# Gla's last two levels of scores as blocks, its small products behind Q's, and retention's out product between the value units

## The chip, the cores and the metric

The program runs on one core of one Trainium2 chip. Its time is the device time of one execution in microseconds (us); lower is better. Five engines work beside each other: TensorE (PE in the profile; PEld is its weight load), VectorE (DVE), ScalarE (ACT), GpSimd (POOL) and SyncE (SP). Each runs its own instructions in order. An instruction that needs another engine's result waits for it, and everything behind it on its engine waits too. Matrix products accumulate in PSUM (8 banks); the other engines read them from there into SBUF.

## The reference

A trunk of two layers over 16 learned meta tokens and 512 tokens of width 1024, all in float32: T = 528 columns. Layer 0 mixes by retention, layer 1 by gated linear attention (gla).

```python
for i in range(DEPTH):                       # DEPTH = 2
    h = h + 0.5 * swiglu(rmsnorm(h, norm_ffn1[i]), ...)
    h = h + Mixer_i(rmsnorm(h, norm_mix[i])) # retention, then gla
    h = h + 0.5 * swiglu(rmsnorm(h, norm_ffn2[i]), ...)
h = rmsnorm(h, final_norm)[:, 16:]
```

Retention has 4 heads with keys of 256 and values of 512; q and k are rotated, the scores decay by a constant for each head, and each head's output is normed, gated by silu(g) and multiplied by its rows of w_out:

```python
q = rotary(q); k = rotary(k) * 256 ** -0.5
S = S * decay_chunk + einsum('bhjd,bhjv->bhdv', k * decay_k, v)
o = scores(q, k, decay) @ v + (q * decay_q) @ S
out = (rmsnorm(o, head_norm) * silu(g)) @ w_out
```

Gla has 4 heads with keys of 128 and values of 256. Its decay is one number for each token and each key channel, made from the input, so that a score is a sum over channels with its own decays:

```python
log_a = log_sigmoid(z @ w_gate + b_gate) / 16
bcum  = cumsum(log_a)                        # in the chunk
s[i, j] = sum_d q[i,d] * exp(bcum[i,d] - bcum[j,d]) * k[j,d]   # j <= i
o = s @ v + (q * exp(bcum)) @ S;  out = (rmsnorm(o, head_norm) * silu(g)) @ w_out
```

## The kernel before

The activations lie transposed, features on the 128 partitions and tokens along a row. A weight tile of 128 x 512 is fetched by SP's DMA (`raw`; two tiles of one unit added to each other by a POOL DMA are a `pair`) and split into a rounded part `whi` (ACT, L141) and the rest `wlo` (DVE, L142). A product is three matmuls for every 128 rows (`mm3`: L366, L367, L368): activations high by weights high, low by high, high by low. ACT and DVE so spend much of their time on splits of weights, which are made some passes ahead of their use, in the order of a plan (`plan_ret`, `plan_gla`) that must follow the order of use.

**Units.** Most projections are units: two weight tiles against two halves of the tokens (2 x 264) in seven passes of twelve matmuls instead of eight, in the order a11, s1, s2, a12, s3, s4, a22. Passes a11, s2, s3 and a22 accumulate in one PSUM bank (`X...`), s1, a12 and s4 in a second tile (`QZ...`). Behind a pass the bank is emptied: after a11, s1 and s2 ACT copies it to a tile `su...` (L561, L559, L565 of before); after s3 DVE makes the unit's lower right quarter, `c22`; after s4 DVE makes its upper row, `row1`; after a22 ACT or DVE makes the lower left quarter, `c21`. Pass a22 writes bank X, so it waits for c22; s2 writes bank X, so it waits for the copy of a11.

**Retention**, for head h of 4: Q's unit (`Xrqkq`, `QZrqkq`) and K's (`Xrqkk`, `QZrqkk`), each followed by its rotation, `rope_pair`: row1 at L1047, c22 at L1050, c21 at L1053 on ACT, and then eight products and splits of 528 columns (L1059 to L1068, L396, L397). Then the out product of head h-1, `out(h - 1)` (`po_r`): normed and gated values (`og`, split into `ogh` and `ogl`) by w_out, eight steps, each added to the residual `x` by DVE (`xa`, L892). Then two value units (`Xrv`, `QZrv`, outputs m0 = 0 and 2), scores (`sc`), turned values (`tv`, a product with the identity), two gate units (`Xrg`), probabilities by values (`po`), and the sums for the norm (`st_ro`). Head 0 has no units in Q, K and the values. The splits and products of `og` of head h-1 (L1258, L396, L397) fall in the time of head h's Q and K units.

**Gla**, for each of two pairs of heads p: Q, K, Km (keys of the meta tokens), then `levels`. Scores with channel decays are made by doubling: at level 0 the diagonal; at level s = 1, 2, 4 ... 64 the second half of each block of 2s tokens is scored against its first half, after which Q's second halves and K's first halves are multiplied by the block's decay (`advance`, tables `tot`; for the meta keys `mt`, `Km`). Each level is a product of whole 128-token tiles, 8 for the pair (`lv`, L1422), of which a mask takes the wanted entries into `Pd` (`copy_predicated`, L1453). Levels 128 and 256 and the meta columns (`lv_m`, from which `PM` comes, L1510) have products of their own. Between levels `filler()` takes one step from a queue, so that TensorE works while DVE advances: eight half steps of the value projection (`gv`, 24 matmuls each), the turned values (`tv`), and two gate projections (`gg`); two more gates stand behind `pv`, the product of probabilities and values (`go`, L1592).

**What sets the order.** The functions issue in program order; a framework then orders each engine's instructions statically by what they wait for and by its own estimates, with `urgent()` raising the evacuations and `issue_after(x)` keeping a block of instructions behind instruction x. The running program doesn't change that order.

Of the kernel before, what the change touches and what calls it, by code (L numbers as in the profile page):

```python
# [16 lines left out]
P = 128  # L17
# [21 lines left out]
RH, RDV = 4, 512  # L39

# [159 lines left out]
def trunk(ctx, tc, a):  # L200
# [55 lines left out]
    def plan_ro(h):  # L256
        for dp in range(4):
            W.add(("ro", h, dp), a["ret_o"][h, dp])

    def plan_ret():  # L260
        for h in range(RH):
            for j in (2 * h, 8 + 2 * h):
                if h:
                    W.add_unit(("rqk", j), a["ret_in"][j], a["ret_in"][j + 1], W.UNIT)
                else:
                    W.add(("rqk", j), a["ret_in"][j])
                    W.add(("rqk", j + 1), a["ret_in"][j + 1])
            if h:
                plan_ro(h - 1)
            for s, o in (("rv", 16), ("rg", 32)):  # L270
                for m in range(0, 4, 2):
                    c = o + 4 * h + m
                    if h == 0 and s == "rv":
                        W.add((s, h, m), a["ret_in"][c])
                        W.add((s, h, m + 1), a["ret_in"][c + 1])
                    else:
                        W.add_unit((s, h, m), a["ret_in"][c], a["ret_in"][c + 1], W.UNIT)
        plan_ro(RH - 1)
# [718 lines left out]
    def retention(feed):  # L997
        with tc.tile_pool(name="retp", bufs=1) as rp, tc.tile_pool(name="wmore", bufs=2) as wp, psum_pool(4) as pp:
# [40 lines left out]
            def head(h):  # L1039
# [65 lines left out]
                def values():  # L1105
                    if h == 0:
                        for m in range(4):
                            w = W.get(("rv", h, m))
                            ps, views = halves_of(f"pv{h}{m}", m)
                            vt.append(rp.tile([P, T], F32, tag=f"gs{m}", name=f"vt{h}{m}"))  # L1110
                            for hf, r in enumerate(HALVES):
                                proj(ps[hf], w, 0, KD, uh, ul, r)
                                if hf == 1:
                                    W.free(w)
                                hook()
                                if m == 3:

                                    renorm(*r)
                            for o, view in views:
                                S.copy(view(vt[m]), o)  # L1120
                            if m == 0 and True:
                                sums(3)
                        return
                    for m0 in (0, 2):
                        vt.extend(rp.tile([P, T], F32, tag=f"gs{m0 + i}", name=f"vt{h}{m0 + i}") for i in range(2))
# [112 lines left out]
                if h:  # L1238
                    out(h - 1)
                if h == 0 and True:  # L1240
                    sums(2)
# [54 lines left out]
    def gla(feed):  # L1296
        with tc.tile_pool(name="glap", bufs=1) as gp, psum_pool(2) as pp:
            other["pool"] = pp
            masks = gp.tile([P, 7, HP], I32, tag="masks", name="masks")
# [107 lines left out]
            def levels(p, filler):  # L1407
# [18 lines left out]

                filler()
# [3 lines left out]
                V.tensor_mul(Qt, Qt, tot)  # L1431
                filler()

                def advance(s, tot, keys=True):
# [3 lines left out]
                    for j in range(2):  # L1438
# [5 lines left out]
                        if keys:  # L1444
                            V.tensor_tensor(kv[:, :, 0, :], kv[:, :, 0, :],
                                            tv[:, :, 1:2].broadcast_to([P, nb, s]), ALU.mult)
                            V.tensor_tensor(new[:, j, :], tv[:, :, 0], tv[:, :, 1], ALU.mult)
# [3 lines left out]
                while s <= 64:  # L1451
                    ps = tile_scores(f"lv{p}_{s}", s)
# [32 lines left out]
                for s in (1, 2, 4, 8):  # L1485
                    nb = NM // (2 * s)
                    for j in range(2):
                        kb = kmv[:, j, :].rearrange("p (n two s) -> p n two s", two=2, s=s)
                        tb = mt[:, j, :].rearrange("p (n two) -> p n two", two=2)
                        V.tensor_tensor(kb[:, :, 0, :], kb[:, :, 0, :], tb[:, :, 1:2].broadcast_to([P, nb, s]), ALU.mult)  # L1490
                    if s < 8:
                        new = gp.tile([P, 2, nb], F32, tag=f"mt{s}", name=f"mt{p}_{s}")
                        for j in range(2):
                            tb = mt[:, j, :].rearrange("p (n two) -> p n two", two=2)
                            V.tensor_tensor(new[:, j, :], tb[:, :, 0], tb[:, :, 1], ALU.mult)
                        mt = new
# [63 lines left out]
            def gate_steps(p):  # L1560
# [3 lines left out]
                for j in range(2):  # L1564
                    for m in range(2):
                        def step(j=j, m=m):
                            w = W.get(("gg", 2 * p + j, m))
                            pg = acc_tile(f"gg{p}{j}{m}")
                            sg = gp.tile([P, 512], F32, tag=f"gsg{m}", name=f"gsg{p}{j}{m}")
                            proj(pg[:, 0, :], w, 0, KD, uh, ul, TOKENS, halves=2)  # L1570
                            W.free(w)
                            hook()
                            V.tensor_mul(sg, pg[:, 0, :], rb[:, NM:])
                            S.activation(sg, sg, AF.Silu)
                            pr["sg"][j, m] = sg
                        steps.append(step)
# [71 lines left out]
            for p in range(2):  # L1648
# [6 lines left out]
                queue.extend(g[:2])  # L1655
# [9 lines left out]
                g[2]()  # L1665
                sp0 = st0()
                g[3]()
# [31 lines left out]
def _constants():  # L1699
# [14 lines left out]
    lmask = [((j >> n) % 2 == 0) & ((i >> n) == (j >> n) + 1) for n in range(7)]  # L1714
# [62 lines left out]
```

## Time and profile before

| | before |
|---|---|
| median of 3 runs | 2091.62 us (2091.03 to 2092.58) |
| profiled execution | 2091.99 us, span 2090.2 us, granted clock 0.999 |
| TensorE busy | 2069.4 us, 99% |
| DVE busy | 1759.3 us, 84% |
| ACT busy | 1166.0 us, 56% |
| retention, K's units and the first out steps in heads 1, 2 and 3 | 456 to 476, 562 to 582 and 667 to 688 us of the span |
| levels of gla, first pair and second pair | 1515 to 1567 us and 1618 to 1669 us |

Times in rows of the timeline are us from the start of the span; a row gives start, duration, engine, line, operation, output and inputs (buffer numbers left out), shape, a count where equal neighbours are drawn together, and in brackets the idle time ahead of it with what ended it. A duration reaches from dispatch to the last write; since instructions of an engine overlap, what one costs its engine is the distance to the next start. The chain of waits is the work that ended last, followed back from the last instruction.

### The profile page before, as it was taken

The page shows a single profiled execution, that of the slowest core. Times are in us where ns is not written, and L with a number is a line of the kernel's source. Part 1 is how long each engine was busy: PE and PEld are TensorE (multiplying, and loading weights), DVE is VectorE, ACT ScalarE, POOL GpSimd, SP SyncE. Part 2 cuts the span into 40 slices and gives each one's busy share as a digit, 9 for nine tenths or more (in the row PEclk, how much of TensorE's full clock was granted, in tenths as well). Part 3 has the DMA queues.
Part 4 walks back from the last instruction along what each step waited for, and adds up shares of the span by engine and source line. Part 5 has one row for each costly group of instructions (what it writes and reads, how often), then busy time and mean ns, then how long its engine had stood idle before and what let it go on. Part 6 is the DMA issues. An engine that isn't in the chain of part 4 may idle for free.

```text
span 2090.2 us, 42458 instructions
## 1 busy us (share of the span) xinstructions
PE 2069.4 (99%) x16218; PEld 2018.0 (97%) x16218; DVE 1759.3 (84%) x3147; ACT 1166.0 (56%) x2257; POOL 197.3 (9%) x168
## 2 busy tenths in 40 slices
PE   8999999999999999999999999999999999999998
PEld 8999999999999999999999999999998987999998
DVE  8988889968686779988889998889775768998886
ACT  5656566554545455656666565666732335666664
POOL 1011111010101000111111011111000000111110
PEclk9999999999999999999999999999999999999999
DMA  7576767354544431776776476676511111586762
GB/s 218 153 195 159 195 177 191 98 146 128 143 131 131 138 102 67 184 193 156 194 188 167 114 179 181 169 190 175 156 66 66 59 69 66 154 217 165 186 179 71
DMA packets 171804, 309.04 MB, mean 148 GB/s; under 512 B 17104, under 2 KB 40016, under 8 KB 171600
## 3 DMA queue, kind: packets, MB, share of 16 engines
q1 hardware_dynamic: 131696, 231.20, 32.7%
q0 software_dynamic: 38896, 71.84, 21.0%
q10 hardware_dynamic: 1008, 3.29, 0.5%
q8 instruction: 127, 2.08, 0.4%
q14 instruction: 77, 0.63, 0.1%
HBM read 304.16 MB, written 2.10 MB: 147 GB/s over the span
## 4 chain that ended last, share of the span: by engine, by line
PE 92%; DVE 4%; ACT 1%; issue 1%; DMA 1%; POOL 0%; SPq 0%; DVEq 0%; POOLq 0%; ACTq 0%
PE po_r L366 1%; PE po_r L367 1%; PE po_r L368 1%; PE lv L1422 1%; DVE wlo L142 1%; PE Xf11o L366 1%; PE Xf20o L366 1%; PE Xf10o L366 1%; PE Xf20o L367 1%; PE Xf11o L367 1%; PE Xf10o L367 1%; PE Xf11o L368 1%; PE Xf20o L368 1%; PE Xf10o L368 1%; PE Xf21o L366 1%
## 5 line engine op out<-in xcount | busy, mean ns | idle before, releaser
L141 ACT CAST whi<-raw 128x512 fp32r<-128x512 f32 (+1 forms) x886 | 523.1, 606 | 539.7 <-DVE raw L147 79.3
L142 DVE TENSOR_TENSOR wlo<-raw,whi 128x512 fp32r<-128x512 f32 (+1 forms) x886 | 580.1, 669 | 152.9 <-ACT whi L141 142.6
L141 ACT CAST whi<-pair 128x512 fp32r<-128x512 f32 (+1 forms) x290 | 174.9, 603 | 120.7 <-DVE pair L147 7.5
L142 DVE TENSOR_TENSOR wlo<-pair,whi 128x512 fp32r<-128x512 f32 (+1 forms) x290 | 192.5, 664 | 7.2 <-ACT whi L141 5.9
L114 POOL DMA_DIRECT2D pair<-in_f_in x75 | 91.1, 1215 | 757.8 <-DVE wlo L142 169.2
L114 POOL DMA_DIRECT2D pair<-in_f_out x48 | 58.1, 1210 | 412.5 <-DVE wlo L142 135.4
L147 DVE TENSOR_TENSOR raw<-pair,raw 128x512 f32<-128x512 f32 (+1 forms) x139 | 92.5, 666 | 2.6
L149 DVE TENSOR_TENSOR raw<-raw,raw 128x512 f32<-128x512 f32 (+1 forms) x139 | 92.4, 665 | 2.5
L366 PE MATMUL po_r<-ogh,whi 128*128 128x264 f32 x256 | 72.9, 285 | 3.2 <-DVE xa L892 3.2
L367 PE MATMUL po_r<-ogl,whi 128*128 128x264 f32 x256 | 72.7, 284 | 0.0
L368 PE MATMUL po_r<-ogh,wlo 128*128 128x264 f32 x256 | 72.5, 283 | 0.0
L114 POOL DMA_DIRECT2D pair<-in_ret_in x20 | 24.3, 1216 | 300.4 <-DVE wlo L142 133.7
L366 PEld LDWEIGHTS po_r<-ogh,whi 128*128 128x128 f32 x256 | 48.1, 188 | 3.8 <-DVE xa L892 3.8
L366 PE MATMUL Xf11o<-hf,whi 128*128 128x264 f32 x176 | 50.9, 289 | 0.2
L366 PE MATMUL Xf20o<-hf,whi 128*128 128x264 f32 x176 | 50.9, 289 | 0.2
L366 PE MATMUL Xf10o<-hf,whi 128*128 128x264 f32 x176 | 50.8, 289 | 0.2
L367 PE MATMUL Xf11o<-hf,whi 128*128 128x264 f32 x176 | 50.0, 284 | 0.0
L367 PE MATMUL Xf10o<-hf,whi 128*128 128x264 f32 x176 | 50.0, 284 | 0.0
L367 PE MATMUL Xf20o<-hf,whi 128*128 128x264 f32 x176 | 50.0, 284 | 0.0
L368 PE MATMUL Xf10o<-hf,wlo 128*128 128x264 f32 x176 | 49.9, 284 | 0.0
L368 PE MATMUL Xf11o<-hf,wlo 128*128 128x264 f32 x176 | 49.9, 284 | 0.0
L368 PE MATMUL Xf20o<-hf,wlo 128*128 128x264 f32 x176 | 49.9, 284 | 0.0
(843 smaller groups left out, 8444.7 us busy)
## 6 DMA issues: line engine op xcount, KB each, us to landing
raw<-in_f_in SPq DMA_DIRECT2D x277, 256.0 KB, 4.3
pair<-in_f_in SPq DMA_DIRECT2D x150, 256.0 KB, 4.6
pair<-in_f_in POOLq DMA_DIRECT2D x75, 512.0 KB, 6.4
raw<-in_f_out SPq DMA_DIRECT2D x80, 256.0 KB, 3.5
raw<-in_ret_in SPq DMA_DIRECT2D x76, 256.0 KB, 3.3
raw<-in_f_out SPq DMA_DIRECT2D x72, 192.0 KB, 2.8
raw<-in_gla_in SPq DMA_DIRECT2D x50, 256.0 KB, 2.6
pair<-in_f_out SPq DMA_DIRECT2D x48, 256.0 KB, 3.5
```

The costliest lines, as they stand in the source:

```text
L114: nc.gpsimd.dma_start(t, aps[2].unsqueeze(1).broadcast_to([P, 2, n]), accum_op=ALU.add)
L141: self.nc.scalar.copy(hi[:, :n], raw)
L142: V.tensor_sub(lo[:, :n], raw, hi[:, :n].bitcast(F32))
L147: V.tensor_add(s2, self.tiles[c][:, 1], self.tiles[c, "a11"])
L149: V.tensor_add(raw, raw, s2)
L366: nc.tensor.matmul(ps, lhsT=lh, rhs=rh, start=start, stop=False, **kw)
L367: nc.tensor.matmul(ps, lhsT=lh, rhs=rl, start=False, stop=False, **kw)
L368: nc.tensor.matmul(ps, lhsT=ll, rhs=rh, start=False, stop=stop, **kw)
L1422: nc.tensor.matmul(ps[:, j, J * P:J * P + n], lhsT=Kt[:, j, J * P:(J + 1) * P], rhs=q, start=(J == 0), stop=(J == 3), skip_group_check=True)
```

## The change

Two parts, one in each mixer.

Retention: `out(h - 1)` moves from behind K's rotation to between the two value units, and its weights move in the plan likewise. The last head's out product stays behind its gates.

Gla: levels 32 and 64 no longer make whole tiles. `block_scores` makes each wanted block by itself, 32 x 32 or 64 x 64, with the block's keys as the weights and the output on the block's own partitions (strips of 32 or 64 columns of TensorE), and ACT copies the blocks of one strip into `Pd` at once; the two masks go. Two fillers stand behind level 0 instead of one. The products of the tables `tot` and of `mt` and `Km` are kept behind Q's product `qm`. The gate projections become half steps of 12 matmuls each: four in the queue, two behind the first `pv`, two more after them. `BLOCKS` is 32, `NMASK` 5.

```diff
             for s, o in (("rv", 16), ("rg", 32)):
                 for m in range(0, 4, 2):
                     c = o + 4 * h + m
+                    if h and (s, m) == ("rv", 2):
+                        plan_ro(h - 1)
...
                     for m0 in (0, 2):
+                        if m0:
+                            out(h - 1)
                         vt.extend(...)
...
                 rope("k")
-                if h:
-                    out(h - 1)
...
+                def block_scores(name, s):
+                    ps = acc_tile(name)
+                    blocks = range(P // (2 * s))
+                    for j in range(2):
+                        for n in blocks:
+                            k0 = 2 * s * n
+                            for J in range(4):
+                                nc.tensor.matmul(ps[k0:k0 + s, j, J * P:J * P + s],
+                                                 lhsT=Kt[:, j, J * P + k0:J * P + k0 + s],
+                                                 rhs=Qt[:, j, J * P + k0 + s:J * P + k0 + 2 * s],
+                                                 start=(J == 0), stop=(J == 3), skip_group_check=True)
+                    for n in blocks:
+                        k0 = 2 * s * n
+                        S.copy(pd_v[k0:k0 + s, :, k0 + s:k0 + 2 * s],
+                               ps.rearrange("p h (J i) -> p (h J) i", i=P)[k0:k0 + s, :, :s])
...
-                V.tensor_mul(Qt, Qt, tot)
-                filler()
+                qm = V.tensor_mul(Qt, Qt, tot)
+                filler(2)
...
-                            V.tensor_tensor(new[:, j, :], tv[:, :, 0], tv[:, :, 1], ALU.mult)
+                            with tc.issue_after(qm.ins):
+                                V.tensor_tensor(new[:, j, :], tv[:, :, 0], tv[:, :, 1], ALU.mult)
...
                 while s <= 64:
+                    if s >= BLOCKS:
+                        block_scores(f"lv{p}_{s}", s)
+                        tot = advance(s, tot)
+                        filler()
+                        s *= 2
+                        continue
...
-                queue.extend(g[:2])
+                queue.extend(g[:4])
...
                 st0 = pv(p, 0)
-                g[2]()
+                run(g[4:6])
                 sp0 = st0()
-                g[3]()
+                run(g[6:])
                 sp0()
```

Lines of the changed kernel are 4 higher than before's up to the levels (L366 becomes L370, L1050 becomes L1054). In the rows that follow, numbers behind a name tell one tile from another; only the first row of each pass is shown on TensorE.

First place: TensorE in retention's head 1, from K's pass s3. Before:

```order
L366 MATMUL Xrqkk_6266<-rth,whi_6147 128x264
L366 MATMUL QZrqkk_6267<-uha,whi_6163 128x264
L366 MATMUL po_r_6417<-ogh_6057,whi_6219 128x264
L366 MATMUL Xrv_6672<-uha,whi_6430 128x264
L366 MATMUL po_r_6448<-ogh_6057,whi_6281 128x264
L366 MATMUL Xrqkk_6266<-rth,whi_6182 128x264
L366 MATMUL po_r_6478<-ogh_6057,whi_6300 128x264
```

Now:

```order
L370 MATMUL Xrqkk_6265<-rth,whi_6147 128x264
L370 MATMUL QZrqkk_6266<-uha,whi_6163 128x264
L370 MATMUL Xrv_6417<-uha,whi_6219 128x264
L370 MATMUL QZrv_6418<-rth,whi_6280 128x264
L370 MATMUL Xrqkk_6265<-rth,whi_6182 128x264
L370 MATMUL Xrv_6417<-rth,whi_6297 128x264
L370 MATMUL QZrv_6418<-uha,whi_6314 128x264
L370 MATMUL Xrv_6417<-rth,whi_6334 128x264
L370 MATMUL QZrv_6418<-uha,whi_6350 128x264
L370 MATMUL Xrv_6417<-rth,whi_6369 128x264
L370 MATMUL po_r_6552<-ogh_6057,whi_6388 128x264
```

The third and fourth pass behind s3 were two steps' worth of the out product (24 matmuls, then two of `Xrv`, then 24 more); now they are a11 and s1 of the value unit, K's a22 (`whi_6182`) comes next, and the rest of the value unit stands between it and the out product.

Second place: DVE and ACT at that spot. DVE before:

```order
L1062 TENSOR_TENSOR raq_6248<-raq_6248,rbq_6249 128x528
L892 SCALAR_TENSOR_TENSOR xa<-po_r_6417,xa 128x528
L1066 TENSOR_TENSOR rtq_6064<-rtq_6064,ropeq_6059 128x528
L1068 TENSOR_TENSOR q_1_6255<-raq_6248,q_1_6254 128x528
L1067 TENSOR_TENSOR rtq_6063<-rtq_6063,rtq_6064 128x528
L142 TENSOR_TENSOR wlo_6376<-raw_6186,whi_6375 128x512
L1050 TENSOR_TENSOR rtk_6265<-Xrqkk_6266,surqkk_6268 128x264
```

DVE now:

```order
L401 TENSOR_TENSOR ogl_6058<-og_6242,ogh_6057 128x264
L1063 TENSOR_TENSOR raq_6247<-rtq_6063,ropeq_6059 128x528
L1065 TENSOR_TENSOR rbq_6248<-rtq_6064,ropeq_6059 128x528
L1064 TENSOR_TENSOR rtq_6063<-rtq_6063,ropeq_6059 128x528
L1066 TENSOR_TENSOR raq_6247<-raq_6247,rbq_6248 128x528
L1070 TENSOR_TENSOR rtq_6064<-rtq_6064,ropeq_6059 128x528
L146 TENSOR_TENSOR wlo_6315<-raw_5877,whi_6314 128x512
L1071 TENSOR_TENSOR rtq_6063<-rtq_6063,rtq_6064 128x528
L1072 TENSOR_TENSOR q_1_6254<-raq_6247,q_1_6253 128x528
L1054 TENSOR_TENSOR rtk_6264<-Xrqkk_6265,surqkk_6267 128x264
```

ACT now:

```order
L1069 CAST q_1_6253<-raq_6247 128x528
L400 CAST q_1_6255<-rtq_6063 128x528
L145 CAST whi_6350<-raw_5877 128x512
L1057 COPY rtk_6264<-Xrqkk_6265 128x264
L565 COPY surv_6419<-Xrv_6417 128x264
L563 COPY surv_6419<-QZrv_6418 128x264
```

K's c22 (the last DVE row of both) keeps its place behind Q's rotation; the `xa` row that stood among it is gone. On ACT the copies of the value unit's a11 and s1 stand right behind K's c21 copy; before, the first of them stood ten rows behind it.

Third place: TensorE in gla's first pair, from level 32 to level 128. Before:

```order
L1422 MATMUL lv_32_20577<-Q_20043,K_20044 128x64 x8
L366 MATMUL gv_20540<-uha,whi_20371 128x264
...
L1422 MATMUL lv_64_20620<-Q_20043,K_20044 128x64 x8
L1548 MATMUL tv_20637<-ident,vt_20326 96x128
L1548 MATMUL tv_20644<-ident,vt_20326 128x128 x2
L366 MATMUL gg_20690<-uha,whi_20468 128x512
L1548 MATMUL tv_20637<-ident,vt_20326 96x128
L1464 MATMUL lv_128_20672<-Q_20043,K_20044 128x128 x2
```

Now:

```order
L1439 MATMUL lv_32_20603<-Q_20043,K_20044 32x32 x16
L1577 MATMUL tv_20629<-ident,vt_20326 96x128
L1577 MATMUL tv_20636<-ident,vt_20326 128x128
L370 MATMUL gg_20681<-uha,whi_20451 128x512
L1577 MATMUL tv_20636<-ident,vt_20326 128x128
L1439 MATMUL lv_64_20664<-Q_20043,K_20044 64x64
L1577 MATMUL tv_20629<-ident,vt_20326 96x128
L1439 MATMUL lv_64_20664<-Q_20043,K_20044 64x64 x3
L371 MATMUL gg_20681<-ula,whi_20451 128x512
L1439 MATMUL lv_64_20664<-Q_20043,K_20044 64x64 x4
L372 MATMUL gg_20681<-uha,wlo_20452 128x512
```

Level 32 is 16 small matmuls instead of 8, level 64 eight small ones in three stretches, and the 24 value matmuls that stood between the two levels have moved up behind level 0.

More of the change, by code (lines that the diff above doesn't have):

```diff
@@ L39 @@
 RH, RDV = 4, 512
+BLOCKS = 32
+NMASK = 5
 NJ = 5
@@ L267, in plan_ret @@
                     W.add(("rqk", j + 1), a["ret_in"][j + 1])
-            if h:
-                plan_ro(h - 1)
             for s, o in (("rv", 16), ("rg", 32)):
@@ L1120, in values @@
                                 S.copy(view(vt[m]), o)
-                            if m == 0 and True:
+                            if m == 0:
                                 sums(3)
@@ L1237, in head @@
                 rope("k")
-                if h:
-                    out(h - 1)
-                if h == 0 and True:
+                if h == 0:
                     sums(2)
@@ L1298, in gla @@
             other["pool"] = pp
-            masks = gp.tile([P, 7, HP], I32, tag="masks", name="masks")
+            masks = gp.tile([P, NMASK, HP], I32, tag="masks", name="masks")
             nc.sync.dma_start(masks, a["lmask"])
@@ L1484, in levels @@
                 kmv = Km_[:, :, :NM]
[L1485 to L1492, printed above, removed]
+                with tc.issue_after(qm.ins):
+                    for s in (1, 2, 4, 8):
+                        nb = NM // (2 * s)
                         for j in range(2):
+                            kb = kmv[:, j, :].rearrange("p (n two s) -> p n two s", two=2, s=s)
                             tb = mt[:, j, :].rearrange("p (n two) -> p n two", two=2)
-                            V.tensor_tensor(new[:, j, :], tb[:, :, 0], tb[:, :, 1], ALU.mult)
-                        mt = new
+                            V.tensor_tensor(kb[:, :, 0, :], kb[:, :, 0, :], tb[:, :, 1:2].broadcast_to([P, nb, s]), ALU.mult)
+                        if s < 8:
+                            new = gp.tile([P, 2, nb], F32, tag=f"mt{s}", name=f"mt{p}_{s}")
+                            for j in range(2):
+                                tb = mt[:, j, :].rearrange("p (n two) -> p n two", two=2)
+                                V.tensor_tensor(new[:, j, :], tb[:, :, 0], tb[:, :, 1], ALU.mult)
+                            mt = new
                 S.copy(Km_[:, :, MR:].rearrange("p h (g i) -> p h g i", i=MR),
@@ L1565, in gate_steps, with step @@
                     for m in range(2):
-                        def step(j=j, m=m):
-                            w = W.get(("gg", 2 * p + j, m))
-                            pg = acc_tile(f"gg{p}{j}{m}")
+                        def step(j, m, half, hold):
+                            if half == 0:
+                                hold["w"] = W.get(("gg", 2 * p + j, m))
+                                hold["ps"] = acc_tile(f"gg{p}{j}{m}")[:, 0, :]
+                            for k in range(KD // 2 * half, KD // 2 * (half + 1)):
+                                mm3(hold["ps"], *W.at(hold["w"], k * P), uh[k][:, NM:], ul[k][:, NM:], k == 0, k == KD - 1)
+                            if half == 0:
+                                hook()
+                                return
+                            W.free(hold["w"])
+                            hook()
                             sg = gp.tile([P, 512], F32, tag=f"gsg{m}", name=f"gsg{p}{j}{m}")
[L1570 to L1573, printed above, removed]
+                            V.tensor_mul(sg, hold["ps"], rb[:, NM:])
                             S.activation(sg, sg, AF.Silu)
                             pr["sg"][j, m] = sg
-                        steps.append(step)
+                        hold = {}
+                        steps.extend(lambda j=j, m=m, half=half, hold=hold: step(j, m, half, hold) for half in range(2))
                 return steps
@@ L1713, in _constants @@
     j, i = np.arange(P)[:, None], np.arange(P)[None, :]
-    lmask = [((j >> n) % 2 == 0) & ((i >> n) == (j >> n) + 1) for n in range(7)]
+    lmask = [((j >> n) % 2 == 0) & ((i >> n) == (j >> n) + 1) for n in range(NMASK)]
     lmask = np.stack([m[:, (i[0] >> n) % 2 == 1] for n, m in enumerate(lmask)], 1).astype(np.int32)
```

## The prediction

> **What bounds the kernel now.** I read the first part of the page, the shares of the chain that ended last, and then the list of what TensorE waited for.
>
> ```profile
> span 2090.2 us, 42458 instructions
> PE 2069.4 (99%) x16218; PEld 2018.0 (97%) x16218; DVE 1759.3 (84%) x3147; ACT 1166.0 (56%) x2257; POOL 197.3 (9%) x168
> PE 92%; DVE 4%; ACT 1%; issue 1%; DMA 1%; POOL 0%; SPq 0%; DVEq 0%; POOLq 0%; ACTq 0%
> PE po_r L366 <- DVE xa L892: 3.2, 3, 1.3
> PE lv L1422 <- DVE Q L1431: 1.0, 1, 1.0
> PE go L1592 <- DVE PM L1510: 0.2, 1, 0.2
> ```
>
> TensorE is busy all the way, so an edit is worth the TensorE time it takes out, plus the waits it removes, minus the waits it makes. Three waits stand where the change works: 3.2 us on three out products, 1.0 us on Q's first product, 0.2 us on PM. They are at most 4.4 us together. DVE's mean of 84% hides that at the places of the 3.2 us it has nothing to spare (start:end and length, then busy us of PE, PEld, DVE):
>
> ```profile
> 667.00:688.00 21.00, 20.02 (x159) 19.47 (x158) 20.87 (x43) 11.63 (x26) 1.23 (x1) 1.00 0.55 158
> ```
>
> DVE works 20.87 of 21.00 us there. Whatever TensorE asks of DVE earlier than before, it waits for.
>
> **Retention: what goes.** The out product moves, so its first waits on the x update (xa) go; all of the 3.2 us is booked as removed.
>
> **Retention: what comes.** By the new order K's last pass (a22, into K's bank X) follows two value passes; before, it followed four passes of the out product and the wait among them. It can start once DVE's c22 (before's L1050) has read bank X. TensorE's timeline in heads 1, 2 and 3:
>
> ```profile
> 466.94 0.28 PE L366 MATMUL po_r<-ogh,whi 128*128 128x264 f32 x1
> 469.86 0.28 PE L366 MATMUL Xrv<-uha,whi 128*128 128x264 f32 x1
> 471.51 0.39 PE L366 MATMUL po_r<-ogh,whi 128*128 128x264 f32 x1 [1.25 <-DVE xa L892]
> 474.53 0.28 PE L366 MATMUL Xrqkk<-rth,whi 128*128 128x264 f32 x1
> 475.86 0.28 PE L368 MATMUL Xrqkk<-rth,wlo 128*128 128x264 f32 x1
> 572.63 0.28 PE L366 MATMUL po_r<-ogh,whi 128*128 128x264 f32 x1
> 678.30 0.28 PE L366 MATMUL po_r<-ogh,whi 128*128 128x264 f32 x1
> ```
>
> From 466.94 to 469.86 are two passes of twelve matmuls, 1.46 each (0.12 a matmul). In head 1 TensorE will thus want bank X at 469.86, where before it came at 474.53. In heads 2 and 3 it is 572.63 + 2.92 = 575.55 and 678.30 + 2.92 = 681.22. DVE's timeline gives the pitch of its rows and where c22 now stands:
>
> ```profile
> 460.21 0.76 DVE L1258 TENSOR_TENSOR og<-gs,bc_ro 128x264 f32<-128x264 f32 x2
> 460.89 1.28 DVE L142 TENSOR_TENSOR wlo<-raw,whi 128x512 fp32r<-128x512 f32 x2
> 462.10 0.77 DVE L397 TENSOR_TENSOR ogl<-og,ogh 128x264 fp32r<-128x264 f32 x2
> 464.42 0.69 DVE L142 TENSOR_TENSOR wlo<-raw,whi 128x512 fp32r<-128x512 f32 x1 [0.88 <-ACT whi L141]
> 468.28 0.70 DVE L1059 TENSOR_TENSOR raq<-rtq,ropeq 128x528 f32<-128x528 f32 x1
> 468.90 0.70 DVE L1061 TENSOR_TENSOR rbq<-rtq,ropeq 128x528 f32<-128x528 f32 x1
> 470.76 0.70 DVE L892 SCALAR_TENSOR_TENSOR xa<-po_r,xa 128x528 f32<-128x528 f32 x1
> 562.49 0.68 DVE L142 TENSOR_TENSOR wlo<-pair,whi 128x512 fp32r<-128x512 f32 x1
> 668.83 0.42 DVE L1258 TENSOR_TENSOR og<-gs,bc_ro 128x264 f32<-128x264 f32 x1
> 683.46 0.42 DVE L1050 TENSOR_TENSOR rtk<-Xrqkk,surqkk 128x264 f32<-128x264 f32 x1
> ```
>
> A 512-wide row costs 0.60 (460.89 to 462.10, two rows), a 264-wide one 0.34 (460.21 to 460.89, two rows), a 528-wide one 0.62 (468.28 to 468.90). DVE is in order, and the new order still keeps Q's rotation ahead of c22.
> Head 1: after the og pair at 460.21 it has 4 rows of 512, 10 of 264 and 7 of 528 ahead of c22: 2.40 + 3.40 + 4.34 = 10.14. From 460.89 that is 471.03, and c22's 0.42 makes 471.45: 1.6 us after 469.86. Before, DVE lost 0.88 on the way, waiting for ACT's half of a split; the weights now come in another order, but nothing brings that split forward, so I keep it: 2.5.
> Head 2: from 562.49, right behind the first row of Q's unit, it has 9 of 512, 16 of 264, 7 of 528: 5.40 + 5.44 + 4.34 = 15.18; c22 ends at 562.49 + 15.18 + 0.42 = 578.09, 2.5 after 575.55.
> Head 3: 8, 16 and 7 rows, 14.58, from 668.83: c22 ends at 683.83, 2.6 after 681.22. Before, c22 started there at 683.46, so DVE gains nothing by the move although the xa rows are gone from in front; splits of value weights take their place.
> Sum 7.6. Bounds: without the 0.88 and with one 0.60 row less in heads 2 and 3, 5.5; with an idle of 0.88 in those as well, 9.4.
>
> A second wait stands right behind. The values' pass s2 needs bank Xrv, which ACT empties, and in the new order ACT has that copy behind K's c21 copy, which waits for the a22 pass. ACT's timeline:
>
> ```profile
> 461.35 0.37 ACT L559 COPY surqkk<-QZrqkk 128x264 f32<-128x264 f32 x1
> 461.62 0.73 ACT L396 CAST ogh<-og 128x264 fp32r<-128x264 f32 x2
> 476.17 0.38 ACT L1053 COPY rtk<-Xrqkk 128x264 f32<-128x264 f32 x1 [0.90 <-PE Xrqkk L368]
> ```
>
> The c21 copy starts 0.31 after the last matmul of its pass does (475.86 to 476.17), the next copy 0.27 later (461.35 to 461.62), and that takes 0.37: 0.95. TensorE notices 0.05 later (xa ends at 471.46, po_r starts at 471.51), and would have gone on after 0.12: 0.9 a head, 2.7 in all; by the order it cannot be hidden by more than a matmul or two, so 2.2 at the least. What is late next is the values' rows, and with them the scores and the turned values; TensorE has the out product between the value units to cover these, so I book nothing.
>
> Retention: -3.2 + 7.6 + 2.7 = **+7.1** (from -3.2 + 5.5 + 2.2 = +4.5 to -3.2 + 9.4 + 2.7 = +8.9).
>
> **GLA: the block scores.** A level of scores over the whole tile, as the chain of waits has it, and a shorter fp32 pass (12 of 88 columns):
>
> ```profile
> 1526.18 1.73 PE lv L1422 x16
> 451.68 0.86 PE st_ro L408 x12
> ```
>
> Sixteen passes cost 1.73, 0.108 each for 128 weight columns; st_ro costs 0.072 for 88. Both are about 0.83 ns a column, so the columns that are loaded set the pace. A level of 32 becomes 32 passes of 32 columns, about 0.028 each, 0.9; that of 64 becomes 16 passes of 64 columns, 0.055 each, 0.9. Four such levels save 4 x 0.83 = 3.3. That the small passes can be that quick, and what it costs to pass between whole tile and strips of columns, has a nearest row in retention's 16-column scores; strips of rows are the dearer neighbour:
>
> ```profile
> 518.98 0.25 PE L366 MATMUL sc<-q,k 128*16 128x16 f32 x1
> 519.09 0.17 PE L367 MATMUL sc<-q,k 128*16 128x16 f32 x1
> 519.12 0.17 PE L368 MATMUL sc<-q,k 128*16 128x16 f32 x1
> 436.65 0.27 PE L367 MATMUL po<-pl,vh 128*128 128x144 f32 x1
> 436.76 0.28 PE L368 MATMUL po<-ph,vl 128*128 128x144 f32 x1
> 436.97 0.27 PE L366 MATMUL po<-ph,vh 16*128 16x16 f32 x1
> 437.10 0.25 PE L367 MATMUL po<-pl,vh 16*128 16x16 f32 x1
> 437.39 0.33 PE L366 MATMUL po<-ph,vh 128*128 128x128 f32 x1
> ```
>
> Inside the strip a matmul takes 0.03 (519.09 to 519.12), which bears the 0.028 out. The first of them takes 0.11 (518.98 to 519.09), no more than a whole matmul of 144 columns (436.65 to 436.76), so by this row a switch is nearly free. For row strips the way in is 0.21 (436.76 to 436.97); inside, one takes 0.13 (436.97 to 437.10), and from the second to the whole matmul after the third it is 0.29 (437.10 to 437.39). Against 0.11 for each of the four that is 0.63 for 0.44, some 0.2 for the way in and out. The new order has eight stretches of blocks (one of 32 and three of 64 for each pair of heads): 0 to 1.6 in all. I take 0.6, nearer to the column row.
>
> The Trainium skill, page TensorEngine Tiling (Array Packing), section Tiling Modes, says that changing the tiling mode, not only the tile, drains TensorE. By that rule the 0.6 would be nearer to 1.6, and the sum 1.0 higher; the row strips above agree with it, the column strip hardly does.
>
> **GLA: the rest.** The DVE rows ahead of Q's product:
>
> ```profile
> 1516.13 0.32 DVE L1447 TENSOR_TENSOR tot<-tot 128x64 f32<-128x64 f32 x2
> 1518.74 1.22 DVE L1429 TENSOR_TENSOR Pd<-lv,ident 128x1024 f32<-128x1024 f32 x1
> 1519.88 1.21 DVE L1431 TENSOR_TENSOR Q<-Q,A 128x1024 f32<-128x1024 f32 x1
> ```
>
> From 1516.13 to 1518.74 stand small products, which now come behind Q's, so Q is ready up to 2.6 us earlier, and a second stretch of value matmuls stands ahead of level 1: the 1.0 us goes. PM's 0.2 goes too, with half a gate in front of it. In return level 64 follows level 32 with only four other rows between (three turned values and a gate matmul, some 0.7 us), while DVE needs two products of 256 columns before the first block: I book 0.3, out of 0 to 1.4 (0.7 for each pair of heads). The four masked copies that DVE no longer makes, and ACT's copies of blocks in their place, are off the path: DVE and ACT have slack in this stretch, and Pd is read at its end.
>
> GLA: -3.3 + 0.6 - 1.2 + 0.3 = **-3.6** (from -4.5 to -3.3 + 1.6 - 1.2 + 1.4 = -1.5).
>
> **The sum.** +7.1 - 3.6 = +3.5. The profiled execution took 2092.0 (span 2090.2), so it would take 2095.5; it lies 0.4 over the median of the runs, 2091.6, so the median becomes **2095.1**. With the bounds, +4.5 - 4.5 = 0 to +8.9 - 1.5 = +7.4: 2091.6 to 2099.0. A measurement of this kernel tells about 0.2%, 4.2 us, from no change: 2087.4 and 2095.8 are the edges, and the forecast lies just inside.
>
> **Rivals.**
> A wider stall (slower). DVE is held in every head as in head 1, and the xa wait comes back at the out product's new place, between the value units, at half of its 3.2: +3.5 + 1.8 + 1.6 = +6.9, 2098.5. For it speaks DVE's 20.87 of 21.00; against it, that the out product's updates now meet no rotation of Q.
> Dear switches. Eight stretches at 0.2, 1.6 instead of 0.6: +4.5, 2096.1. The row strips speak for it, the 16-column row against it. The rule of the Trainium skill (TensorEngine Tiling (Array Packing), Tiling Modes) is what would bring this case about.
> Half a stall. Where DVE runs freely ahead of its rows of before by some 1.5 us a head, the three stalls lose 4.5: -1, 2090.6.
> No stall (faster). The place is again K's a22 pass: if c22 ends by 469.8, 575.5 and 681.2, that is 1.6 to 2.6 us earlier than I count, the 7.6 falls away and the second wait remains: -0.5 - 3.6 = -4.1; without that as well -6.8: 2084.8 to 2087.5, about 2087. It decides from about 2 us a head. For it speaks only that Q's rotation waits for nothing on TensorE; against it, the full DVE of the window.
> That blocks save nothing (32 passes at 0.108) I hold for excluded by the 0.03 row; it would add 2.6 a level of 32 and 0.8 a level of 64, 6.8 in all.
>
> **How the numbers follow.** Forecast 0.45 (0.28 under 2095.8, 0.17 over), wider stall 0.16 (slower), dear switches 0.12 (0.04 same, 0.08 slower), half a stall 0.15 (same), no stall 0.12 (faster). Same 0.47, slower 0.41, faster 0.12. The range from 2089 to 2099 takes in the bounds and half a stall and leaves out the faster case and the far end of the wider stall; the forecast's own is 2093 to 2097.
>
> **What would show it.** In the list of TensorE's waits: xa's 3.2 gone; K's bank X on DVE's c22 with three waits of about 2.5; Xrv on ACT's copy with three of about 0.9; Q's 1.0 gone. In the source view the block passes at 0.03 and 0.055, and ten masked copies for fourteen. It is wrong if K's a22 waits less than 1 us a head, if xa is still waited for, or if level 64 waits over 1 us for Q.

## The result

The change makes the kernel slower: 1.0032 of the time before (95% interval 1.0021 to 1.0042), 2098.9 us median (2098.24 to 2102.61) against 2092.85 in runs beside it (2091.03 to 2094.69). That is +6.7 us by the ratio; the two profiled executions lie 6.9 apart (2098.9 and 2092.0; spans 2097.1 and 2090.2). The forecast was +3.5 and no change that can be told. The two parts went in opposite directions, and the loss was larger than counted.

The head of the page of the changed kernel, with its chain's shares:

```profile
span 2097.1 us, 42534 instructions
PE 2069.2 (99%) x16250; PEld 2015.2 (96%) x16250; DVE 1755.1 (84%) x3143; ACT 1167.9 (56%) x2263; POOL 197.3 (9%) x168
PE 88%; DVE 8%; issue 1%; ACT 1%; DMA 1%; POOL 0%; SPq 0%; DVEq 0%; POOLq 0%; ACTq 0%
```

And what its TensorE waited for (us in total, times, longest):

```profile
PE Xrqkk L370 <- DVE rtk L1054: 7.1, 3, 2.5
PE Xrv L370 <- ACT surv L565: 2.1, 3, 0.8
PE po_r L370 <- DVE xa L896: 1.7, 1, 1.7
PE sc L370 <- DVE pl L401: 0.6, 3, 0.2
```

TensorE's work is the same, 2069 us; DVE's share of the chain that ended last went from 4% to 8%. K's bank X on c22 and Xrv on ACT's copy stand there as forecast, three times each. The 3.2 us on xa are gone from their old places, but 1.7 us on xa are new. The waits on Q and on PM are gone from gla.

Two stretches of TensorE's timeline say what each part did. The first goes from the same pass of head 1's Q unit to the norm's sums of head 3 (st_ro), the second from gla's norm (st_n) to the sums of its second pair (st_go). Before:

```profile
447.12 0.28 PE L366 MATMUL QZrqkq<-rth,whi 128*128 128x264 f32 x1
745.59 1.03 PE L408 MATMUL st_ro<-ones,osq 128*88 128x1 f32 x12
1485.44 1.25 PE L475 MATMUL st_n<-ones,sqa_n 128*128 128x1 f32 x10
1686.40 0.95 PE L408 MATMUL st_go<-ones,gs 128*128 128x1 f32 x8
```

After:

```profile
447.40 0.28 PE L370 MATMUL QZrqkq<-rth,whi 128*128 128x264 f32 x1
755.51 1.03 PE L412 MATMUL st_ro<-ones,osq 128*88 128x1 f32 x12
1495.88 1.25 PE L479 MATMUL st_n<-ones,sqa_n 128*128 128x1 f32 x10
1693.45 0.95 PE L412 MATMUL st_go<-ones,gs 128*128 128x1 f32 x8
```

Retention takes 308.11 instead of 298.47: **+9.6**. Gla takes 197.57 instead of 200.96: **-3.4**. The remaining 0.6 lies outside: 0.3 ahead of head 1, 0.5 between the two stretches, less 0.2 won back behind them.

### The profile page after: what moved, and what is told of

Its sections match the earlier page's. It is cut to its first block, busy times and chain, and to the rows that moved or that the text cites. A ratio compares the mean times of both kernels' runs of the same rounds, so it can differ in the third digit from the quotient of the medians.

```text
span 2097.1 us, 42534 instructions
## 1 busy us (share of the span) xinstructions
PE 2069.2 (99%) x16250; PEld 2015.2 (96%) x16250; DVE 1755.1 (84%) x3143; ACT 1167.9 (56%) x2263; POOL 197.3 (9%) x168
## 4 chain that ended last, share of the span: by engine, by line
PE 88%; DVE 8%; issue 1%; ACT 1%; DMA 1%; POOL 0%; SPq 0%; DVEq 0%; POOLq 0%; ACTq 0%
DVE wlo L146 2%; PE po_r L370 1%; PE po_r L371 1%; PE po_r L372 1%; PE Xf11o L370 1%; PE Xf20o L370 1%; PE Xf20o L372 1%; PE Xf11o L371 1%; PE Xf11o L372 1%; PE Xf20o L371 1%; PE lv L1426 1%; PE Xf21o L370 1%; PE Xf20u L370 1%; PE Xf11u L370 1%; PE Xf20u L371 1%
## 5 line engine op out<-in xcount | busy, mean ns | idle before, releaser
L153 DVE TENSOR_TENSOR raw<-raw,raw 128x512 f32<-128x512 f32 (+1 forms) x139 | 92.6, 666 | 2.5
L370 PE MATMUL po_r<-ogh,whi 128*128 128x264 f32 x256 | 72.7, 284 | 1.9 <-DVE xa L896 1.7
L370 PE MATMUL Xf20o<-hf,whi 128*128 128x264 f32 x176 | 50.9, 289 | 0.2
L370 PE MATMUL Xf11o<-hf,whi 128*128 128x264 f32 x176 | 50.9, 289 | 0.2
L370 PE MATMUL Xf10o<-hf,whi 128*128 128x264 f32 x176 | 50.9, 289 | 0.2
L370 PEld LDWEIGHTS po_r<-ogh,whi 128*128 128x128 f32 x256 | 48.2, 188 | 2.2 <-issue 2.2
```

What stands on the lines that cost most here:

```text
L153: V.tensor_add(raw, raw, s2)
L370: nc.tensor.matmul(ps, lhsT=lh, rhs=rh, start=start, stop=False, **kw)
```

## The experiments

All in one table first; retention and gla are the two stretches above, each from one profiled execution, as difference to before.

| run | ratio (95%) | retention | gla |
|---|---|---|---|
| the change | 1.0032 (1.0021 to 1.0042) | +9.64 | -3.39 |
| e1, gla part alone | 0.9983 (0.9974 to 0.9992) | +0.63 | -3.31 |
| e2, out product moved alone | 1.0061 (1.0048 to 1.0074) | +12.00 | +0.09 |
| e3, change, K's own tiles | 0.9989 (0.9980 to 0.9998) | +1.43 | -3.26 |
| e4, change, c21 on DVE | 1.0030 (1.0018 to 1.0041) | +10.81 | -3.26 |
| e5, e3 with the larger stock | 0.9961 (0.9948 to 0.9973) | -3.48 | -3.35 |
| e6, own tiles and move in heads 1, 2 | 0.9971 (0.9960 to 0.9983) | -2.32 | -3.37 |
| e7, gla part without blocks | 0.9985 (0.9975 to 0.9994) | +0.99 | -2.06 |
| e8, gla part, blocks at 64 only | 0.9987 (0.9978 to 0.9996) | +1.25 | -2.40 |
| e9, e5 with the old place | 0.9968 (0.9957 to 0.9980) | -2.87 | -3.32 |
| e10, change with the larger stock | 1.0041 (1.0026 to 1.0056) | +10.51 | -3.39 |

How far a single execution can be trusted stands in the table too. In e1, e7 and e8 TensorE, DVE and ACT have the same retention instructions in the same order as before, and yet retention takes 0.6 to 1.3 us longer. So a difference under 1.3 us in the retention column tells nothing by itself. The gla column repeats better: the eight runs with the whole gla part lie between -3.26 and -3.39.

**The two parts apart.** e1 is the changed kernel with the out product and its weights back in their old places; e2 is the kernel before with these two moved.

> The change's gla part alone, retention as before. Theory: gla gains what the two traces show behind retention, 3 to 3.6 us (offset of the two spans +10.4 at gla's start, +6.9 at the end), so 0.9983 of before, and the three waits of TensorE on xa (3.2 us) stay. Rival: the two parts are not separate (retention's delay lets DVE and the weights run ahead, and gla's gain is borrowed from it): 0 to 1 us gained, ratio over 0.9995.

> The move of the out product alone, gla as before. Theory: the loss is 9.5 to 10.5 us, ratio 1.0046 to 1.0050, with K's bank X waiting on c22 three times at 2.3 to 2.6 us, Xrv on ACT's copy three times, and one wait on xa in head 1. Rival: parts not separate, loss near the whole change's 6.9, ratio 1.0033.

The parts are separate: e1 gains in gla what the whole change gains there, and its three waits on xa stay (3.5 us). e2's list of waits has 7.1 on c22, 2.2 on Xrv and 1.6 on xa, as the whole change has them, but its retention lost 12.0, not 9.6. The 2.4 more all lie in head 2 and stand on no list of waits; they are in the last section.

**Why c22 is late.** The prediction took DVE's order as given. The code has a reason for it: K's unit writes into two tiles of the tag `sg`, which has two buffers, and these are the two tiles in which Q's rotation still works. c22 can't be ordered ahead of the rotation's last read. e3 gives K's unit tiles of its own, in the two buffers that the second value unit uses later:

```diff
-t = [tmp.tile([P, T], F32, tag="sg", name=f"rt{s}{h}{m}") for m in range(2)]
+t = [tmp.tile([P, T], F32, tag="sg", name=f"rt{s}{h}{m}") if s == "q" else
+     rp.tile([P, T], F32, tag=f"gs{2 + m}", name=f"rt{s}{h}{m}") for m in range(2)]
```

> The whole change, but K's unit in heads 1 to 3 writes into two tiles of its own (the buffers that the second value unit uses later) instead of the two in which Q's rotation still works. Theory: c22 stands behind Q's rotation because it writes over the rotation's tile, not because DVE is short of time; with tiles of its own DVE has c22 ten rows earlier in head 1, K's a22 hardly waits (under 0.5 us a head instead of 2.4), and the ACT copies that wait behind c21 go with it. Retention then gains up to 3.7 of before and gla 3.5: 4.5 to 7 us faster than before, 0.9967 to 0.9979. Rival: DVE is full (20.9 of 21 us), whatever comes earlier puts something else late: the 7.1 turns up at og, the splits or the scores, and the run stays at before or over it, ratio 1.000 to 1.003.

DVE's timeline of head 1, the changed kernel:

```profile
466.58 0.71 DVE L1063 TENSOR_TENSOR raq<-rtq,ropeq 128x528 f32<-128x528 f32 x1
470.89 0.71 DVE L1072 TENSOR_TENSOR q<-raq,q 128x528 fp32r<-128x528 f32 x1
471.51 0.44 DVE L1054 TENSOR_TENSOR rtk<-Xrqkk,surqkk 128x264 f32<-128x264 f32 x1
```

And with K's own tiles:

```profile
465.95 0.43 DVE L1055 TENSOR_TENSOR rtk<-Xrqkk,surqkk 128x264 f32<-128x264 f32 x1
467.73 0.70 DVE L1064 TENSOR_TENSOR raq<-rtq,ropeq 128x528 f32<-128x528 f32 x1
472.04 0.70 DVE L1073 TENSOR_TENSOR q<-raq,q 128x528 fp32r<-128x528 f32 x1
```

c22 goes ahead of the rotation, 5.6 us earlier, and neither K's bank X nor xa is on e3's list of waits any more. But the whole gained only 0.9989, half of what the theory said. Head 1's Q unit started 0.33 us later than before, head 3's 2.0 us earlier: 2.3 gained in two heads. Head 3 then lost 3.8. The rival was right there. What e3's TensorE waited for:

```profile
PE Xrv L372 <- DVE wlo L146: 1.5, 1, 1.5
PE po_r L370 <- ACT whi L145: 0.5, 1, 0.5
```

And DVE's timeline of its head 3:

```profile
686.27 0.71 DVE L1071 TENSOR_TENSOR rtk<-rtk,ropek 128x528 f32<-128x528 f32 x1
686.89 0.69 DVE L146 TENSOR_TENSOR wlo<-pair,whi 128x512 fp32r<-128x512 f32 x1
```

The splits of the value unit's weights (wlo) stand among the rows of K's rotation, and TensorE waits for them. About 1.4 of the 3.8 are not the waits themselves: behind them TensorE ran at half its clock for 3.4 us (last section). Head 3 has fewer of these splits in store: the kernel takes its two extra split tiles away at the start of the last head and splits 4 ahead instead of 8. e5 takes them away only behind the values; e6 keeps heads 1 and 2 of e3 and puts the last head back as it was before the change. The edit of e5:

```diff
             for h in range(RH):
-                if h == RH - 1:
-                    W.less()
                 head(h)
...
                 values()
+                if h == RH - 1:
+                    W.less()
```

> As the run with K's own tiles, but the last head keeps the stock of split weights of the other heads (8 splits ahead and two tiles more) until its values are done, where before it went down to 4 ahead at its start. Theory: the 3.8 us that the last head lost in the run with K's own tiles come from the small stock there, so that DVE's two rotations hold up the splits of the value unit; with the larger stock the last head loses under 0.5 us and the whole stands 5 to 6 us under before, 0.9971 to 0.9976. Rival: DVE is full and the splits come late with any stock: the last head still loses 2 to 4, 0.9983 to 0.9992.

> The whole change, with K's own tiles in heads 1 and 2, and the last head as it was before the change (out product behind K's rotation, shared tiles). Theory: heads 1 and 2 keep what they gained in the run with K's own tiles (1.5 and 0.85 us by the offsets of the two timelines), the last head is as before, gla gives 3.3: 5 to 6 us under before, 0.9971 to 0.9976. Rival: what heads 1 and 2 gain is only borrowed from DVE and comes back as a longer wait on xa in the last head (over 1.0 us): 3.3 us, 0.9984.

e6 came out by its theory. e5 went further than its own, 8.2 us by the ratio where 5 to 6 were said: its last head lost nothing but gained 1.2 on the last head of before. In e5 none of the waits on c22, on Xrv's copy or on xa is left, retention is 3.48 under before, and the whole, 0.9961 at 2084.75 us median (2084.42 to 2086.08) and a span of 2082.6, beats the kernel before and the changed one. e6's -2.32 is what e3 had gained in heads 1 and 2, and its last head is as long as before's, with one wait of 1.0 on xa.

e10 is e5 without the own tiles, so the change with the stock alone:

> The whole change with the larger stock in the last head and nothing else (K's unit in the shared tiles). Theory: the stock alone doesn't help, since c22 waits for its tile, not for a split: K's bank X still waits three times, 7 us in all, and the time stays 5.5 to 8 us over before, 1.0026 to 1.0038. Rival: the stock does it in the last head, one of the three waits shrinks by over 1.5 us, and the time falls to 3 to 5 us over before, 1.0014 to 1.0024.

The three waits on c22 are there again, 7.1 us. Stock without tiles is worth nothing. Tiles without stock are worth 8.2 of the 13.1 us that lie between the change and e5 in retention.

**Is the new place worth anything?** e9 is e5 with the out product and its weights back behind K's rotation.

> The gla part, K's own tiles and the larger stock in the last head, but the out product in its old place behind K's rotation. It tells whether the move is worth anything once its stalls are gone. Theory: the move is what removes the waits on xa; here they stay, 2.5 to 3.5 us, and the time is that of the gla part alone, 2.5 to 4 us under before, 0.9981 to 0.9988. Rival: the tiles and the stock are the gain, and the place doesn't matter: xa's waits are under 1 us and the time is within 1.5 us of the run with the move, 0.9961 to 0.9968.

The theory fell: there is no wait on xa in e9, and it stands only 0.6 us behind e5 in retention (-2.87 against -3.48; the medians, 2086.49 and 2084.75, were measured apart and differ by 1.7, and the intervals of the two ratios overlap). By heads, the old place is 0.4 ahead in heads 1 and 2 together and 1.0 behind in the last. The sum is inside what single executions with the same instructions differ by, so that the move is worth anything beside tiles and stock is not shown. TensorE of e9 in head 1:

```profile
466.64 0.28 PE L370 MATMUL po_r<-ogh,whi 128*128 128x264 f32 x1
467.77 0.39 PE L370 MATMUL Xrqkk<-rth,whi 128*128 128x264 f32 x1
469.32 0.28 PE L372 MATMUL po_r<-ogh,wlo 128*128 128x264 f32 x1
```

With c22 early, K's a22 pass slips in among the first out step and pushes the later steps back by its 1.5 us, and xa's wait is covered. So in heads 1 and 2 the waits on xa of before were, like those on c22 of after, a consequence of the shared tiles; in the last head e9 has the larger stock too, and which of the two removes the wait there wasn't tried.

**The copy behind c21.** e4 makes K's c21 copy on DVE:

```diff
 def c21(c):
-    S.copy(t[1][:, a0:a1], c)
+    (S.copy if s == "q" else V.tensor_copy)(t[1][:, a0:a1], c)
```

> The whole change, but K's c21 copy in heads 1 to 3 is made by DVE instead of ACT. Theory: the wait of Xrv on ACT's copy of a11 comes from that copy standing behind c21 on ACT; it goes (2.1 us by the list of waits, up to 2.9 by TensorE's steps), the 7.1 on c22 stays, DVE has 0.34 more a head: 4 to 5.5 us slower than before, 1.0020 to 1.0026. Rival: TensorE would wait there for the a11 copy or the weights anyway, and the time stays at the change's +6.9, 1.0032.

The time, 1.0030, can't be told from the change's. On the list the wait of Xrv shrank from 2.1 to 1.4 and that of xa from 1.7 to 0.8, but the profiled execution lost more than that in a way that the last section tells. And the copy came no sooner. ACT's copy of a11 in head 1, in the changed kernel and in e4:

```profile
474.10 0.39 ACT L565 COPY surv<-Xrv 128x264 f32<-128x264 f32 x1
474.20 0.37 ACT L565 COPY surv<-Xrv 128x264 f32<-128x264 f32 x1
```

K's a22 starts at 472.00 in the one and at 471.89 in the other, so the copy stands 2.1 and 2.3 us behind it. The wait is gone from head 1 of e4 because TensorE ran at half its clock there (472.6 to 476.0) and wanted the bank later. In head 3, at full clock, it is 1.0 against 0.8. ACT's timeline there shows what stands ahead of the copy:

```profile
693.04 1.14 ACT L145 CAST whi<-raw 128x512 fp32r<-128x512 f32 x2 [1.62 <-DVE raw L153]
694.09 0.37 ACT L565 COPY surv<-Xrv 128x264 f32<-128x264 f32 x1
```

Two splits of weights stand before the copy, and the first waits for DVE's sum of two weight tiles (L153), which itself stands behind c22. The late c22 holds ACT that way too. In e3 the whole wait went with the tiles. So the rival was right.

**Gla in pieces.** e7 sets `BLOCKS` to 128 and `NMASK` to 7 in e1, e8 to 64 and 6.

> The gla part alone without its blocks: seven levels by whole tiles and masks, but the fillers, the order of the small products and the half gates as changed. Theory: only the waits on Q and PM go, 1.2 us between gla's start and its end on the timeline, ratio about 0.9994; the blocks are the other 2.1 of the 3.3. Rival: the new order of fillers is the gain, 2.5 to 3.3 us without the blocks, 0.9984 to 0.9988.

> The gla part alone with blocks at level 64 only; level 32 by whole tiles and a mask. Theory (switches cost some 0.2 us a stretch, three stretches a level 64, one a level 32): level 64 is worth little, some 0.4 us a pair of heads by the steps of its 16 passes, 1.2 + 0.7 = 1.9 us in gla, and level 32 the rest of 3.3. Rival (switches free): both levels are worth 0.83 a pair, less what is common: 1.2 + 1.05 to 1.65 = 2.3 to 2.9 us.

e7 lies between its theory and its rival: without blocks the part already gains 2.06, 0.85 more than the theory's 1.2. e8's 2.40 lies in its rival's range, but only because of that 0.85: from e7 on, level 64's blocks add 0.34 (the theory said 0.7) and level 32's 0.91, 1.25 together for two pairs of heads. These steps are read from one stretch of one execution each; the whole times of e7 and e8 can't be told apart. The price of the switches is in the timeline of the changed kernel's first pair:

```profile
1557.39 0.90 PE L1439 MATMUL lv<-Q,K 128*32 128x32 f32 x32
1558.22 0.42 PE L1577 MATMUL tv<-ident,vt 128*96 128x128 f32 x2
1558.40 0.48 PE L370 MATMUL gg<-uha,whi 128*128 128x512 f32 x1
1558.72 0.27 PE L1577 MATMUL tv<-ident,vt 128*128 128x128 f32 x1
1558.93 0.32 PE L1439 MATMUL lv<-Q,K 128*64 128x64 f32 x2
1559.18 0.31 PE L1577 MATMUL tv<-ident,vt 128*96 128x128 f32 x1
1559.42 0.56 PE L1439 MATMUL lv<-Q,K 128*64 128x64 f32 x6
1559.92 0.49 PE L371 MATMUL gg<-ula,whi 128*128 128x512 f32 x1
1560.34 0.68 PE L1439 MATMUL lv<-Q,K 128*64 128x64 f32 x8
1560.95 0.50 PE L372 MATMUL gg<-uha,wlo 128*128 128x512 f32 x1
1561.28 0.40 PE L370 MATMUL gg<-uha,whi 128*128 128x512 f32 x1
1561.52 0.39 PE L371 MATMUL gg<-ula,whi 128*128 128x512 f32 x1
```

Level 32's 32 passes take 0.83, 0.026 each: less than counted. Level 64's take 0.25, 0.50 and 0.61 for 2, 6 and 8, 1.36 instead of 0.88, so each stretch costs 0.16 to its end. The row ahead of a stretch is longer too: the gate matmul at 1559.92 takes 0.42 to the next start, while one ahead of a turned value takes 0.32 (1558.40 to 1558.72); the turned-value matmul at 1559.18 takes 0.24, where the prediction's rows have 0.11 for a whole matmul. That is 0.10 to 0.13 more, some 0.3 a stretch of 64 in all.

The 0.85 that e7 gains beyond the waits on Q and PM is in short steps ahead of and behind small products (turned values, the first rows of go), which no list of waits names. Which part of the new order gives it wasn't tried.

## Why the prediction was wrong, step by step

- **That retention's stalls outweigh gla's gain** was right in sign and mechanism, as far as the three waits on c22 and the three on ACT's copy go. The size was 3.4 short: 2.5 in retention, 0.2 in gla, and the rest outside the two stretches, where the sum has no term.
- **K's a22 on c22, 7.6.** Right: 7.1 on the list of waits; by TensorE's steps from the last value matmul (2.34, 2.81 and 2.81, each less 0.12) 7.6. Counting DVE's rows of the new order with durations from before gave the three waits to 0.3 us, and the "half a stall" and "no stall" rivals fell with it. The reason was incomplete. The prediction named DVE's full order ("Whatever TensorE asks of DVE earlier than before, it waits for"); it was a shared buffer that forced the order, since with tiles of its own c22 came 5.6 us earlier and the waits were gone (e3), and DVE's fullness decided only in the last head (e3 against e5).
- **Xrv on ACT's copy, 2.7.** 2.1 on the list, 2.9 by TensorE's steps (1.09, 0.46 and 0.77, and 1.04, each less 0.12 for a matmul); place and size were right. That the copy is late because it stands behind c21 was wrong: without c21 ahead of it, it came as late (e4).
- **"All of the 3.2 us is booked as removed."** This is the step that failed first. 1.7 came back in head 1, behind the third of its eight out steps, where TensorE waits for the update (xa) of the second; and "if xa is still waited for" was the prediction's own sign of being wrong. The "wider stall" rival had 1.6 for this. Its total, 2098.5, comes nearest to what was measured, but by luck: its other half, 1.8 more on c22, did not come. The chain of waits of the changed kernel there, in extract:

```profile
476.96 4.06 DMA raw<-in_ret_o
481.57 0.61 ACT whi L145
483.46 0.61 DVE wlo L146
484.13 5.66 DMA raw<-in_ret_in
489.81 0.63 ACT whi L145
490.46 1.29 DVE wlo L146 x2
491.76 0.63 DVE xa L896
```

  xa stands behind a split that waited for a weight tile; that tile's load could start only when an earlier split, late itself, had freed a buffer. e3 and e5 keep the same weights in the same order without the stall, and xa doesn't wait in them. So the stall caused it by way of the weights, on a queue that the prediction didn't follow; no run changed that queue alone.
- **"TensorE has the out product between the value units to cover these, so I book nothing."** The second failed step: from the first wide scores (sc, 128x400) to the next head's Q unit, heads 1 and 2 take 0.4 us longer each. In head 1 the offset to before grows from 3.7 to 4.1. The list of waits has 0.6 for sc where before had 0.2. In every run with the new place in heads 1 and 2 (e2 to e6, e10) both heads take the same 0.4 longer there, with the stalls or without, and with the old place (e1, e7, e8, e9) neither does. So this belongs to the new place itself.
- Together, all by TensorE's steps in the two profiled executions: the old waits on xa were 3.7, c22 is 7.6, Xrv 2.9, the new wait on xa 1.9, and behind the scores 0.8. -3.7 + 7.6 + 2.9 + 1.9 + 0.8 = 9.5, of 9.6 measured. The two steps booked at nothing, 2.7, are the 2.5 that were missing; the small misses in the other terms cancel.
- **Gla, -3.6.** -3.4: right by two errors that cancel. The waits and the order were worth 2.06 instead of 0.9 (1.2 less the 0.3 booked; level 64 never waited for Q), and the blocks 1.25 instead of 2.7. The switches were booked at 0.6, "nearer to the column row"; they cost some 2 us, eight stretches at about 0.26 (the 3.3 saved in the passes less the 1.25 left). The row strips, at some 0.2 each, were the better neighbour. The Trainium skill (TensorEngine Tiling (Array Packing), Tiling Modes) says that a change of tiling mode drains TensorE; these rows agree with it. The 16-column strip that argued against it was a poor neighbour; why it switches more cheaply wasn't tried.
- **The range** (2089 to 2099) held the time at its very end; the likeliest case's own range (2093 to 2097) did not. The likeliest outcome, no change that can be told (0.47), did not come: the measured interval lies wholly on the slower side.

## What to carry to other kernels

When a step is moved so that an evacuation (a copy that empties a PSUM bank) is asked for earlier, look for what keeps the evacuation from coming earlier. Here that was not the engine's load but a target buffer that another step was still using. Two spare tiles, with a larger stock of splits in the last head, were the gain; that the move adds anything to them was not shown. A stall that is booked as removed is safe only when the queues behind its releaser (the splits, their loads, the buffers these free) have been followed through the new place as well. Cutting a matmul into strips pays for few long stretches: a stretch of 64-column blocks cost about 0.3 us in switches here, as much as five of its passes.

## What the runs showed of the hardware that was not expected

A stall can cost more than its length. In e2 head 2 has the same waits as in the changed kernel, 2.5 us on c22 and then a copy, but behind the first of them TensorE ran at half its clock. A window of e2 (start:end and length; busy us of PE, PEld, DVE, ACT, POOL; then the granted clock):

```profile
582.60:590.50 7.90, 7.29 (x35) 6.98 (x36) 7.28 (x12) 3.20 (x8) 1.22 (x1) 0.57 0.78 199
```

The same stretch of the changed kernel's profiled execution:

```profile
582.00:592.00 10.00, 8.97 (x69) 8.58 (x70) 9.66 (x17) 5.20 (x12) 1.22 (x1) 1.00 0.75 191
```

And rows of e2 from inside it. From start to start a matmul of this kind takes 0.12 ahead of 583.5 and 0.22 behind it:

```profile
582.58 0.39 PE L366 MATMUL Xrqkk<-rth,whi 128*128 128x264 f32 x1 [2.53 <-DVE rtk L1050]
582.81 0.28 PE L367 MATMUL Xrqkk<-rtl,whi 128*128 128x264 f32 x1
582.93 0.28 PE L368 MATMUL Xrqkk<-rth,wlo 128*128 128x264 f32 x1
583.58 0.42 PE L367 MATMUL Xrqkk<-rtl,whi 128*128 128x264 f32 x1
583.80 0.42 PE L368 MATMUL Xrqkk<-rth,wlo 128*128 128x264 f32 x1
585.93 0.59 PE L366 MATMUL Xrv<-rth,whi 128*128 128x264 f32 x1 [0.61 <-ACT surv L561]
```

The granted clock is 0.50 from 583.5 to 590.2. Some 24 matmuls at 0.1 us more are the 2.4 us that e2 lost beyond the change, and no wait names them. The same was seen in e3's head 3 (0.50 from 687.4 to 690.7), in e4's heads 1 and 2, and in e10's head 3, each behind such waits, and nowhere in the retention of e5, e6 and e9, which have no wait over 1.0 us there. Near the start of e1 and e7 it followed waits of 1.4 and 1.7 us. Which execution has it varies: over the nine runs of the changed kernel the mean granted clock goes from 0.999 at 2098.24 us to 0.996 at 2102.61.

The Trainium skill (TensorE: Matmul & The Clock Gate, Part 1: The HAM clock gate) describes a gate that halves the array's clock after an idle window of about 3.4 us, freely running, and that opens again after as long a busy one. The half clock and its varying appearance agree, and so does the length of the slow stretches, 3.4 us in e3, e4 and e10 and twice that in e2. But no idle stretch of 3.4 us was needed: in e2 it was one wait of 2.5. In the 3.4 us just ahead of a slow stretch in retention TensorE was busy for 0.9 us (e2), 1.5 (e3), 1.3 and 1.1 (e4) and 1.4 (e10). Cut into such pieces, counted back from the clock's fall at the end of the run, no piece of the changed kernel's retention has less than 1.7. That would explain why the same waits cost speed in one execution and not in the next. It is a reading of these few cases and was not tested, and the two at the start don't fit it (2.2 us in e1, 1.8 in e7). All five runs of e2 have a low mean clock (0.994 to 0.997); whether they lost it at the same place, and why every one did, stays open.
